# A hybrid encoder block: the order of its stages turned round, input projections first

## The chip, the cores and the metric

The kernel runs on one core of a Trainium2 chip. The metric is the device time in microseconds of one execution. TensorE (PE) multiplies, VectorE (DVE), ScalarE (ACT) and GpSimd (POOL) do the elementwise work, SyncE (SP) issues the weight loads. Each engine works through its own instruction stream; semaphores join them.

## The reference, cut to what matters

One residual block on x of 512 tokens by 2048 features, in float32:

```
h    = rms_norm(x, norm_g)
proj = h @ w_in          # split into c, b, u, conv_z (1024 each), c_q 512, c_kv 512, k_rope 64,
                         # mla_z 2048, mem_q 1024, mem_z 1024, g_conv, g_mla, g_mem (2048 each)
o_conv = (b * conv3(c * u) * silu(conv_z)) @ w_conv_out
q  = rms_norm(c_q) @ w_uq;  k, v = rms_norm(c_kv) @ w_ukv      # 16 heads, 128 + 64 rotary
mla_y = attention(q, k, v, chunk mask)
o_mla = (mla_y * silu(mla_z)) @ w_mla_out
mk, mv = rms_norm(mem, mem_norm_g) @ w_mem_kv                  # mem: 256 tokens, 4 heads of 256
mem_y = attention(rms_norm(mem_q), rms_norm(mk), mv)
o_mem = (mem_y * silu(mem_z)) @ w_mem_out
merged = sigmoid(g_conv)*o_conv + sigmoid(g_mla)*o_mla + sigmoid(g_mem)*o_mem
out = x + merged @ w_o
```

## The kernel before

**How a product is made.** Every float32 operand is cut into a high part (`hi`, an ACT copy to the type fp32r, L121) and a low part (`lo`, a DVE subtraction, L123, or with a gain L125). `mm3` (L152 to L154) makes one product of three matmuls: hi by hi, hi by lo, lo by hi. A weight chunk is 256 rows by 512 columns (512 KB, tile `raw`); its cut takes one ACT and one DVE instruction of 128x1024. All sums of a product collect in PSUM banks; there are four under the tag `acc` and four under `aux`.

**Dense products** (`dense_steps`, later `d_group`) take one chunk at a time for four token blocks: 24 matmuls with 512 columns for a chunk, 192 for 512 output columns of a 2048-row weight. The latents c_kv use chunks of 288 columns.

**Block products** (`f_group`, `t_group`) are a two-by-two block scheme with seven products in place of eight (P1 to P7). DVE forms sums and differences of the weight blocks before they are cut, and of the result blocks afterwards. `f_group` gives 512 features by all tokens in 14 steps of 24 matmuls with 256 columns; `t_group` gives 1024 columns by all tokens in 28 steps of 12 matmuls with 512 columns. Both read `BX`, the blocks of the normalised x: their parts `b0` and `b1` and the sums `f`, cut like everything else.

**The stages, in order.**
1. Memory keys and values: `w_mem_kv`, 4 groups of 8 chunks, two token blocks each, so 12 matmuls of 512 columns a chunk. `memory_chunk` loads and cuts mem, `add_squares` on POOL (L241, L245) sums the squares. Meanwhile x is loaded, and `make_hT` scales it on POOL (L303), cuts it (`hT`) and stores it to `hdram`.
2. The latents: `w_ckv0`, `w_ckv1` (288 columns each), `w_cq`, from `hT`.
3. Latent attention: `project` makes keys, values and queries of two heads, `attend` is a generator for one head. The strings `ORDER_FIRST`, `ORDER` and `ORDER_LAST` say in which order a step of `project` (p), of a head (0, 1) or of the previous head (L) is written. The result is copied (L675) to `ydram`.
4. The memory query `w_memq`, a dense product; h comes back from `hdram`. Then memory attention, two heads after each half of the query product (`mem_queries`, `mem_attend`, L742 to L800).
5. `w_memz`, a dense product; `build_x` makes BX between its steps.
6. Block products: 8 conv groups and 4 `w_mlaz` groups (`f_group`; `mlaz_group` multiplies with the attention result from `ydram`, L1176), then 6 gate groups (`t_group`).
7. The output side: `w_mem_out` (dense), `w_mla_out` (block), `w_conv_out` (dense), `w_o` (block).

**What sets the order.** From stage 5 on, `steps` is a list: each step cuts its weights (`forms`), then multiplies, then runs what hangs on it (`after`); the cut of the next step is written ahead of the `after` of this one. On PE, ACT, DVE and POOL a planner orders the instructions at compile time by costs that it simulates, with the written order as priority; SP keeps the written order (`manual_schedule`):

```
ctx.enter_context(tc.manual_schedule(engines={mybir.EngineType.SP}))
...
with tile.TileContext(nc, schedule_with_timeline_sim=True) as tc, ExitStack() as ctx:
```

Tiles of one tag share a few buffers; a write waits until the old content is used.

## Time and profile before

| | us |
|---|---|
| median of 3 runs | 2172.26 (2170.84 to 2175.69) |
| the profiled execution, time | 2173.34 |
| its span, first to last instruction | 2171.5 |
| PE busy | 2120.9 |
| weight loads of PE busy | 1857.2 |
| DVE busy | 1586.1 |
| ACT busy | 1024.2 |
| POOL busy | 213.1 |

The span is what the engines took from the first instruction to the last; the time holds 1.8 us more around it. A busy time is the time in which at least one instruction of the engine ran, so span less busy is idle time. A row of stretches gives the length, then for each engine the busy time and the count of instructions, then the granted clock of PE as a share of full speed, the busy share of the DMA engines, and what they moved.

### The profile page before, as it was taken

What the parts mean: (1) busy time and instruction counts of PE and PEld (TensorE: products, weight loads), DVE (VectorE), ACT (ScalarE), POOL (GpSimd) and SP (SyncE); (2) the same over time, 40 slices, a digit from 0 to 9 for tenths busy, and PEclk for the clock granted to TensorE, in tenths of its full rate; (3) what the DMA queues carried; (4) which work ended last, traced back from release to release, by engine and by line L of the source; (5) the groups of instructions that cost most, each with busy time, mean ns of one, the idle gap of its engine ahead of it and who ended that gap; (6) DMA issues with size and microseconds to landing.
All of it is one profiled execution on the core that took longest, in us unless ns stands there. A gap on an engine that the chain in (4) does not pass through costs nothing.

```text
span 2171.5 us, 30437 instructions
## 1 busy us (share of the span) xinstructions
PE 2120.9 (98%) x11832; PEld 1857.2 (86%) x11832; DVE 1586.1 (73%) x2101; ACT 1024.2 (47%) x1509; POOL 213.1 (10%) x211
## 2 busy tenths in 40 slices
PE   6999999999989999999999999999999999999999
PEld 5788888888868899999999988888888888888887
DVE  7863767774457578778777877777787678777986
ACT  5533667675344344444444444444455434443443
POOL 7510311210000000000000000000001100021000
PEclk9999999999999999999999999999999999999999
DMA  7583212234225332332454454544456666585662
GB/s 264 156 258 111 88 49 64 69 127 166 76 70 202 127 116 90 127 122 84 145 165 157 146 181 128 195 164 166 154 204 212 237 240 190 188 243 163 208 230 78
DMA packets 103679, 334.29 MB, mean 154 GB/s; under 512 B 11120, under 2 KB 11376, under 8 KB 103536
## 3 DMA queue, kind: packets, MB, share of 16 engines
q1 hardware_dynamic: 73008, 256.51, 36.0%
q0 software_dynamic: 12864, 43.00, 6.3%
q10 hardware_dynamic: 17664, 32.86, 4.0%
q8 instruction: 92, 1.51, 0.3%
q14 instruction: 51, 0.42, 0.1%
HBM read 284.09 MB, written 48.23 MB: 153 GB/s over the span
## 4 chain that ended last, share of the span: by engine, by line
PE 68%; DVE 1%; issue 1%; DMA 1%; ACT 1%; POOL 0%; ACTq 0%; DVEq 0%; POOLq 0%
PE aux L152 12%; PE aux L154 12%; PE aux L153 12%; PE acc L153 10%; PE acc L154 10%; PE acc L152 10%; DMA araw<-adram 1%; DVE wlo L123 0%; PE aux L203 0%; ACT p L777 0%; PE acc L203 0%; ACT whi L121 0%; DVE qrow L746 0%; POOL mdram L1338 0%; DVE r L1232 0%
## 5 line engine op out<-in xcount | busy, mean ns | idle before, releaser
L121 ACT ACTIVATE whi<-raw 128x1024 fp32r<-128x1024 f32 x472 | 499.8, 1060 | 700.7 <-PE aux L153 310.2
L123 DVE TENSOR_TENSOR wlo<-raw,whi 128x1024 fp32r<-128x1024 f32 x472 | 575.4, 1223 | 277.8 <-ACT whi L121 277.1
L146 DVE TENSOR_TENSOR wlo<-raw,whi 128x1024 fp32r<-128x1024 f32 (+3 forms) x105 | 128.9, 1228 | 112.6 <-ACT whi L145 112.2
L962 DVE TENSOR_TENSOR raw<-raw 128x1024 f32<-128x1024 f32 x160 | 195.6, 1223 | 8.6 <-DMA raw<-in_w_mla_out 2.7
L145 ACT ACTIVATE whi<-raw 128x1024 fp32r<-128x1024 f32 (+3 forms) x105 | 101.2, 964 | 141.0 <-PE acc L154 71.8
L154 PE MATMUL acc<-whi,blk 128*128 128x512 f32 (+1 forms) x384 | 144.4, 377 | 0.0
L153 PE MATMUL acc<-wlo,blk 128*128 128x512 f32 (+1 forms) x384 | 144.2, 376 | 0.0
L152 PE MATMUL acc<-whi,blk 128*128 128x512 f32 (+1 forms) x384 | 142.1, 384 | 2.1 <-DVE qt L584 1.4
L153 PE MATMUL aux<-wlo,f 128*128 128x512 f32 x320 | 124.5, 389 | 0.0
L154 PE MATMUL aux<-whi,f 128*128 128x512 f32 x320 | 124.5, 389 | 0.0
L152 PE MATMUL aux<-whi,f 128*128 128x512 f32 x320 | 113.2, 389 | 0.5 <-ACT E L1366 0.5
L196 POOL TENSOR_TENSOR rs_r<-rs_t,mhalf 128x2 f32<-128x2 f32 (+1 forms) x77 | 69.5, 907 | 287.7 <-DVE rs_t L195 202.2
L908 DVE TENSOR_TENSOR raw<-raw 128x1024 f32<-128x1024 f32 x72 | 87.1, 1222 | 1.4
L152 PEld LDWEIGHTS acc<-whi,blk 128*128 128x128 f32 x384 | 72.4, 189 | 14.2 <-ACT kn L562 2.2
L154 PE MATMUL acc<-f,wlo 128*128 128x256 f32 x288 | 81.6, 283 | 1.6 <-DVE wlo L123 1.6
L153 PE MATMUL acc<-f,whi 128*128 128x256 f32 x288 | 81.5, 283 | 0.0
L152 PE MATMUL aux<-f,whi 128*128 128x256 f32 x288 | 81.5, 283 | 0.0
L153 PE MATMUL aux<-f,whi 128*128 128x256 f32 x288 | 81.5, 283 | 0.0
L154 PE MATMUL aux<-f,wlo 128*128 128x256 f32 x288 | 81.5, 283 | 0.0
L152 PE MATMUL acc<-f,whi 128*128 128x256 f32 x288 | 81.5, 283 | 0.0
L154 PEld LDWEIGHTS acc<-whi,blk 128*128 128x128 f32 x384 | 72.5, 189 | 10.2
L153 PEld LDWEIGHTS acc<-wlo,blk 128*128 128x128 f32 x384 | 72.7, 189 | 9.4
(405 smaller groups left out, 5937.9 us busy)
## 6 DMA issues: line engine op xcount, KB each, us to landing
raw<-in_w_conv SPq DMA_DIRECT2D x64, 512.0 KB, 3.8
raw<-in_w_mla_out SPq DMA_DIRECT2D x44, 512.0 KB, 4.7
raw<-in_w_o SPq DMA_DIRECT2D x44, 512.0 KB, 4.3
raw<-in_w_gmem SPq DMA_DIRECT2D x40, 512.0 KB, 3.6
raw<-in_w_gconv SPq DMA_DIRECT2D x40, 512.0 KB, 3.8
raw<-in_w_gmla SPq DMA_DIRECT2D x40, 512.0 KB, 4.3
raw<-in_w_mlaz SPq DMA_DIRECT2D x32, 512.0 KB, 3.9
raw<-in_w_mem_kv SPq DMA_DIRECT2D x31, 512.0 KB, 3.7
```

Source lines behind the costliest of these rows:

```text
L121: act.activation(hi, src, AF.Copy, scale=1.0 if g is None else g)
L123: vec.tensor_tensor(out=lo, in0=src, in1=r32(hi), op=ALU.subtract)
L145: act.activation(hi[:, cols], raw[:, cols], AF.Copy)
L146: vec.tensor_tensor(out=lo[:, cols], in0=raw[:, cols], in1=r32(hi[:, cols]), op=ALU.subtract)
L152: nc.tensor.matmul(o, lhsT=s[0], rhs=m[0], start=start, stop=False, skip_group_check=shared)
L153: nc.tensor.matmul(o, lhsT=s[0], rhs=m[1], start=False, stop=False, skip_group_check=shared)
L154: nc.tensor.matmul(o, lhsT=s[1], rhs=m[0], start=False, stop=stop, skip_group_check=shared)
L196: pool.tensor_tensor(out=r, in0=t, in1=mhalf[:, :n], op=ALU.pow)
L908: vec.tensor_tensor(out=src_, in0=fetch(i0), in1=fetch(i1), op=op)
L962: vec.tensor_tensor(out=src_, in0=src_, in1=fetch((gid, other, c)), op=op)
```

## The change

The stages stand in a new order, and two products change their kind.

- x is loaded first. Its unscaled chunks, times the gain, are cut (`x_chunk`) and go straight into both c_kv products, interleaved by chunk (`kv_forms`, `kv_products`), and into c_q. The scale of a token is a factor of a whole row of these latents, so it is left out there, and the norms of the latents take a corrected epsilon (`xe`). The latents are stored to `ckvdram`, `krdram`, `cqdram`.
- The sum of squares of x is made by ACT and DVE (`x_squares`), `make_scale` turns it into the scale, and `build_x` makes BX between the steps of c_q, on DVE.
- All block products follow: gate group 0 first (with the `lead` order, in which the fourth chunk comes last; it loads four chunks twice), conv, the other gates, `w_mlaz`, and now also `w_memz` (`f_group`) and `w_memq` (`t_group`), which were dense. Their results go to DRAM (`zdram`, `mzdram`, `mqdram`).
- Memory keys and values come next; the memory tokens are loaded and cut during the last gate group (`mem_load`, `mem_cut`, `mem_sum`). The four memory heads are generators now, and their parts hang between the 32 steps (`go`), as do the rotary tables, the loads of the latents and their scales.
- Then latent attention. `attend` loads its gate z (POOL queue) and multiplies the result with it on DVE in place of the ACT copy; `mlaz_group`'s multiplication is gone.
- The last heads are interleaved with the first steps of `w_mem_out` instead of with the memory query.
- `hdram`, `ydram`, `mydram` and their transfers are gone. Weights of all stages share one ring (`w`, ten buffers; before, four in the first stages).

The diff, cut to its core:

```diff
-    making = make_hT()
-    for grp in range(4):
-        banks = [bank("acc") for _ in range(2)]
-        for c, _ in enumerate(dense_steps(banks, a["w_mem_kv"][grp], 512, mT, "T", nk=KB, cut=grp == 0,
-                                          before=memory_chunk if grp == 0 else None)):
...
+    def x_chunk(c):
+        t = xraw[c] = q("xraw")
+        hi, lo = (blk("xhi"), blk("xlo")) if c < 4 else (b1("xhi"), b1("xlo"))
...
+        for k in range(KC):
+            split(t[:, k], hi[:, k], lo[:, k], g(G_NORM + KC * c + k))
+            hx[KC * c + k] = (hi[:, k], lo[:, k])
+    def x_squares(c):
+        sq = q("sq")
+        act.activation(flat(sq), flat(xraw[c]), AF.Square)
+        if c:
+            vec.tensor_tensor(out=flat(xacc[0]), in0=flat(xacc[0]), in1=flat(sq), op=ALU.add)
...
+    for c in range(8):
+        for n in range(2):
+            steps.append(Step(lambda n=n, c=c: kv_forms(n, c), [lambda ws, n=n, c=c: kv_products(ws, n, c)],
+                              [lambda n=n: kv_results(n)] if c == 7 else []))
...
+    def build_x(c):
+        for j in (c, c + 4):
+            for k in range(KC):
+                t = xraw[j][:, k]
+                vec.scalar_tensor_tensor(out=t, in0=t, scalar=g(G_NORM + KC * j + k), in1=scale[0],
+                                         op0=ALU.mult, op1=ALU.mult)
+        build(BX, c, xraw[c], xraw[c + 4], blk)
+    first = len(steps)
+    after(first - 1, make_scale)
+    d_group(a["w_cq"], hx, "aux", q_results, "F", order=(0, 4, 1, 5, 2, 6, 3, 7))
+    for c in range(4):
+        after(first + 2 * c + 1, lambda c=c: build_x(c), True)
...
+    gate_group(0, 0, True)
+    for cb in range(8):
+        f_group(a["w_conv"][cb], BX, conv_group(cb), "aux" if cb % 2 else "acc")
+    gate_group(0, 1)
+    for grp in range(4):
+        f_group(a["w_mlaz"][grp], BX, z_group(zdram, 4 * grp), "aux" if grp % 2 else "acc")
+    gate_group(1, 0)
+    gate_group(1, 1)
+    for grp in range(2):
+        f_group(a["w_memz"][grp], BX, z_group(mzdram, 4 * grp), "aux" if grp % 2 else "acc")
+    t_group(a["w_memq"][0], BX, rows_group(mqdram, 0, AF.Copy))
+    gate_group(2, 0)
+    last_s = len(steps)
+    gate_group(2, 1)
...
+    for grp in (0, 2, 1, 3):
+        d_group(a["w_mem_kv"][grp], mT, "acc", mem_results(grp), "T", nb=2)
+    after(first_m - 1, mem_sum)
...
+    def mem_attend(head):
+        rows = pq.tile([P, NTB, M], F32, tag="rows", name="rows", bufs=2)
+        nc.gpsimd.dma_start(rows, mqdram[:, :, head * M:(head + 1) * M].rearrange("t p f -> p t f"))
+        yield
...
+    for s, h in ((0, 0), (1, 0), (2, 1), (8, 0), (9, 1), (11, 0), (12, 1), (14, 1), (16, 0), (17, 1), (17, 2), (18, 3),
+                 (19, 2), (24, 2), (25, 3), (27, 2), (28, 3), (30, 3)):
+        after(first_m + s, go(h))
+    for s, f in ((3, rotary_tables), (20, latent_loads), (22, key_scales), (23, key_rotary), (26, query_scale)):
+        after(first_m + s, f)
...
+    query_blocks()
+    for h in range(2, 4):
+        for _ in heads_m[h]:
+            pass
+    key_blocks()
...
+    run_all(queries(0, res0))
+    run_all(keys_values(0, res0, "aux"))
...
     def attend(head, h, qrb, res):
+        z = pa.tile([P, S], F32, tag="z", name="z", bufs=3)
+        nc.gpsimd.dma_start(z, zdram[head])
...
-        y = pa.tile([P, S], F32, tag="y", name="y", bufs=2)
-        act.activation(y, yb, AF.Copy)
-        (nc.gpsimd if head >= HEADS - 4 else nc.scalar).dma_start(ydram[head], y)
+        vec.tensor_tensor(out=z, in0=yb, in1=z, op=ALU.mult)
+        (nc.gpsimd if head >= HEADS - 4 else nc.scalar).dma_start(adram[16 + head], z)
...
+    late_steps = run_range(first_o, len(steps))
+    a0, a1 = prev
+    run(*[{"p": late_steps, "L": late, "0": a0, "1": a1}[c] for c in ORDER_LAST])
...
-    a["w_memq"] = groups(w_in, 7232, 1024)
-    a["w_memz"] = groups(w_in, 8256, 1024)
+    a["w_memq"] = two_by_two_t(w_in[:, 7232:8256])[None]
+    a["w_memz"] = np.stack([two_by_two(w_in, [(8256 + i * 512, 512)]) for i in range(2)])
```

## The prediction

> **What bounds the kernel now.** I read the page first: busy times, then the chain that ended last.

> ```profile
> span 2171.5 us, 30437 instructions
> PE 2120.9 (98%) x11832; PEld 1857.2 (86%) x11832; DVE 1586.1 (73%) x2101; ACT 1024.2 (47%) x1509; POOL 213.1 (10%) x211
> PE 68%; DVE 1%; issue 1%; DMA 1%; ACT 1%; POOL 0%; ACTq 0%; DVEq 0%; POOLq 0%
> ```

> PE is the bound. It is idle for 2171.5 - 2120.9 = 50.6 us, so a reordering can win at most that plus whatever PE work it removes. The view of stretches, cut at the stages, shows where the idle time lies:

> ```profile
> core 0: us, PE busy (x) PEld busy (x) DVE busy (x) ACT busy (x) POOL busy (x), PEclk, DMA share, GB/s
> 0.00:36.00 36.00, 21.83 (x82) 16.33 (x82) 28.15 (x29) 18.64 (x29) 23.37 (x20) 0.95 0.72 258
> 36.00:117.00 81.00, 72.89 (x324) 56.17 (x324) 66.76 (x63) 46.97 (x71) 49.98 (x28) 1.00 0.58 185
> 117.00:160.00 43.00, 41.53 (x291) 39.60 (x290) 24.95 (x54) 15.47 (x28) 3.19 (x2) 1.00 0.85 274
> 208.00:470.00 262.00, 256.39 (x1416) 226.43 (x1415) 189.31 (x556) 177.26 (x430) 56.88 (x62) 0.99 0.21 68
> 470.00:565.00 95.00, 91.78 (x484) 78.66 (x483) 49.53 (x131) 50.26 (x123) 11.28 (x14) 1.00 0.48 169
> 613.00:648.00 35.00, 25.22 (x117) 19.32 (x116) 19.45 (x46) 14.41 (x43) 4.27 (x6) 0.85 0.21 70
> 648.00:736.00 88.00, 87.27 (x385) 72.27 (x386) 51.29 (x68) 32.32 (x45) 3.37 (x5) 1.00 0.50 179
> 736.00:1059.00 323.00, 321.44 (x2679) 321.24 (x2678) 259.30 (x256) 141.18 (x153) 0.99 (x2) 1.00 0.36 114
> ...
> 1378.00:1531.00 153.00, 153.00 (x677) 126.69 (x676) 118.13 (x107) 72.71 (x75) 0.00 (x0) 1.00 0.50 167
> 1922.00:2012.00 90.00, 89.16 (x418) 74.20 (x417) 62.12 (x71) 35.13 (x45) 9.95 (x13) 1.00 0.63 209
> 2012.00:2171.50 159.50, 154.34 (x688) 127.16 (x686) 129.34 (x124) 66.30 (x71) 5.78 (x8) 1.00 0.51 172
> ```

> Length less PE busy, from the top: 14.2, 8.1, 1.5 (memory keys, then latents), 5.6 (latent attention), 3.2 (its end), 9.8 (the last two memory heads), 0.7, 1.6, 0, 0.8, 5.2 (output side and tail). Together 50.7: all of it. The clock column adds a loss that busy time hides: 25.22 x 0.15 + 21.83 x 0.05 = 4.9 us at a lower clock. Who PE waited for:

> ```profile
> PE acc L153 <- DVE wlo L146: 17.0, 16, 4.2
> PE acc L152 <- ACT whi L145: 6.8, 4, 5.8
> PE aux L203 <- DVE p L782: 4.2, 4, 1.9
> PE aux L203 <- DVE qrow L746: 2.4, 3, 1.3
> ```

> The largest is the weight cut at the start, the others are memory heads that stand alone. Why DVE is late there, its timeline and POOL's say:

> ```profile
> 17.95 2.06 DVE L146 TENSOR_TENSOR wlo<-raw,whi 128x1024 fp32r<-128x1024 f32 x1
> 30.36 1.21 DVE L146 TENSOR_TENSOR wlo<-raw,whi 128x1024 fp32r<-128x1024 f32 x1
> 18.89 3.67 POOL L245 TENSOR_TENSOR macc<-macc,sq 128x512 f32<-128x512 f32 x2
> ```

> The same cut takes 2.06 us while POOL sums squares and 1.21 us after it has stopped.

> **PE work.** Matmuls of 512 columns follow each other every 87.27/385 = 0.2267 us (the memory gate's stretch; 153/677 = 0.226 in the gates'), those of 256 columns every 321.44/2679 = 0.120. The memory gate `w_memz` goes from 2 x 192 x 0.2267 = 87.0 to 2 x 336 x 0.120 = 80.6: **-6.4**. The memory query goes from 87.0 to 336 x 0.2267 = 76.2: **-10.9**. An eighth less work gives the gate only a fourteenth, because in the conv stretch the weight loads (PEld) are busy for 321.24 of 323 us: with 256 columns a matmul is paced by its weights. [...] The scales of memory and of the latent queries take eight one-column matmuls more:

> ```profile
> 35.30 0.95 PE L264 MATMUL aux<-one,macc 128*128 128x1 f32 x8
> ```

> That is +0.9. All other products keep count and shape. Work: **-16.4**.

> **The start.** One 256 KB transfer, one cut, one matmul, as before: 5.8 us idle (the 5.8 of L145) stays. Then per chunk PE has 48 matmuls of 288 columns, started here nine matmuls apart:

> ```profile
> 129.87 0.30 PE L154 MATMUL acc<-whi,hT 128*128 128x288 f32 x1
> ...
> 131.05 0.29 PE L153 MATMUL acc<-wlo,hT 128*128 128x288 f32 x1
> ```

> That is 0.131 each, 6.3 us a chunk. It loads 1.1 MB, 174 GB/s, where 117 to 160 us moved 274 at 1.5 us of PE idle. DVE prices:

> ```profile
> L123 DVE TENSOR_TENSOR wlo<-raw,whi 128x1024 fp32r<-128x1024 f32 x472 | 575.4, 1223 | 277.8 <-ACT whi L121 277.1
> L123 DVE TENSOR_TENSOR f<-t,f 128x512 fp32r<-128x512 f32 x36 | 23.9, 686 | 0.1
> L146 DVE TENSOR_TENSOR wlo<-raw,whi 128x576 fp32r<-128x576 f32 x16 | 12.1, 757 | 24.2 <-ACT whi L145 24.1
> L1160 DVE SCALAR_TENSOR_TENSOR r<-cu,gains,r 128x512 f32<-128x512 f32 x8 | 6.0, 746 | 0.0
> ```

> DVE needs 2 x 0.746 + 2 x 0.757 + 1.22 = 4.2 us a chunk, without POOL beside it: hidden. I take 0.5 idle (0 to 4).

> **c_q and BX.** PE has 192 x 0.2267 = 43.5 us. DVE has four builds, each 4 x 0.746 (scale) + 4 x 0.69 (sums) + 2 x 1.22 + 3 x 0.686 (cuts) = 10.2, and eight weight cuts: 50.6. It starts some 5 us late, behind the chain sum, power, transposes, copy; three cuts are made ahead (six buffers). DVE then runs about 50.6 + 5 - 3.7 - 43.5 = 8 us past PE, and steps queued behind a build (the third, fifth, seventh cut) hold PE. The lead order, which wants the fourth chunk last, gives some back. Lower end 0 if the planner puts cuts ahead of builds, upper end 12; I take **5**. Before, the builds lay in the memory gate's 87 us with 51.29 of DVE: free.

> **Block groups.** Gate groups (DVE 118.13 of 153) and conv (259.30 of 323) ran with 0 and 1.6 idle and keep their form; `w_mlaz` loses its multiplications. 1.6 stays.

> **Memory stage.** 32 steps are 384 x 0.2267 = 87.1 of PE. A head is 24 x 0.120 + 12 x 0.2267 + 16 transposes. Rows that price heads:

> ```profile
> 579.32 1.04 PE L203 MATMUL aux<-ident,p 128*128 128x128 f32 x8
> L195 DVE TENSOR_SCALAR rs_t<-ss,ke 128x2 f32<-128x2 f32 x32 | 7.3, 242 | 0.3
> L771 DVE TENSOR_REDUCE mx<-aux 128x2 f32<-128x512 f32 x8 | 5.5, 690 | 4.4 <-PE aux L154 4.3
> 565.00:613.00 48.00, 48.00 (x248) 40.85 (x248) 18.99 (x34) 17.81 (x37) 0.00 (x0) 1.00 0.12 39
> ```

> So 7.7 us a head, 118 for the stage. DVE: cuts 39; a head 1.22 + 2 x (0.75 + 0.69 + 0.69 + 0.34 + 0.69 + 0.69) = 8.9, so 36; keys and values 12; tables and scales some 70 small ones at about 0.24 = 17: 104, or 88%. From 565 to 613 two heads lay between dense steps with no PE idle, but steps there last twice as long. Lower end 0, upper end 12 (1.22 x 10 late cuts); I take **4**, for 9.8 before.

> **Into latent attention.** All eight `blk` tiles hold memory features until the last memory step, so the latents' cuts wait for it; and the keys of groups 0 and 1 share the four `aux` banks, so the second waits for an eviction through ACT, DVE and POOL. Cover is the last heads' 24 matmuls (5.4 us) and 16 transposes (2.1). 0 to 10, taken: **5**. Before, this seam was free.

> **Latent attention and its end.** The gate's multiplication adds 16 x 0.69 = 11 to DVE: 200 of 262, still covered. Sixteen z loads join POOL's queue; the powers queue behind each, and DVE's normalisation waits for those:

> ```profile
> L1093 POOL DMA_DIRECT2D adram<-y x4 | 2.9, 728 | 75.0 <-DVE y L1092 75.0
> L196 POOL TENSOR_TENSOR rs_r<-rs_t,mhalf 128x2 f32<-128x2 f32 x44 | 35.4, 811 | 151.4 <-DVE rs_t L195 149.8 <-ACT sq L243 1.3
> ```

> 16 x 0.73 = 12 us on an engine busy for 57 of 262: PE idle stays 5.6. The end, now against `w_mem_out`: 2.5 for 3.2 (0 to 7). Output side and tail: 0.8 + 5.2. SP is moved past nothing it waits for: its loads have ten buffers in place of four, and 16.8 MB to and from `hdram` are gone.

> **The sum.** Idle after: 5.8 + 0.5 + 5 + 1.6 + 4 + 5 + 5.6 + 2.5 + 0.8 + 5.2 = 36.0, for 50.6: -14.6. Lower clock: 4.9 before, an estimate of 1.5 after (one start): -3.4. Work -16.4. Together -34.4: span 2137.1, and 1.8 around it (2173.34 - 2171.5) 2138.9. The profiled run lies 1.1 above the median of the runs, so **2138**.

> **Rivals.** *The seams close*: the planner fills all five new seams (0.5, 5, 4, 5, 2.5): 2138 - 17 - 1.5 of clock = 2119. For it: 565 to 613. Against it: DVE at 50.6 for 43.5 in c_q is no matter of order. *The seams gape*: c_q 10, memory 12, the two ends 10 and 5, so 20 more: 2158; or 34 more, no change, 2172. For it: 9.8 idle in 35 us at memory heads. *Slower*: POOL and DVE disturb each other in the memory stage, as from 17.95 to 22 us. DVE is at 104 for PE's 118, so a slowdown beyond 1.13 decides; at 2.06/1.21 = 1.7 it takes 177, 59 more: 2197. [...] Against it: only about 20 us of POOL (powers and DMA issues at 0.73 to 0.81) lie in those 118 us, and conv's cuts kept 1.22 beside loads. The break-even with 2172 is a slowdown of 1.46. That the products stay dense is ruled out by the diff.

> **How the numbers follow.** Forecast 0.50, seams close 0.15, seams gape but less than the gain 0.20, gain eaten 0.06, slower 0.09. The range 2117 to 2164 leaves out the last two and a little of each edge. A measurement here tells 0.2% (4.3 us) from no change; so faster 0.85, same 0.06, slower 0.09.

> **What would show it.** Right: conv-like pitch (0.120) in `w_memz`; first cuts at 1.22; PE idle under 10 us up to the end of c_q beyond the start; a memory stage near 118 us. Wrong: cuts of 2 us in the memory stage, a PE wait over 5 us on the first gate group, or a clock under 0.9 at the seam into latent attention.

## The result, and the profile after

The changed kernel takes 2153.68 us (median of 4 runs, 2153.02 to 2155.12) where the kernel before took 2171.99 beside it (4 runs, 2170.84 to 2175.69): a ratio of 0.9914, 95% interval 0.9897 to 0.9931. It is faster by 18.3 us. The forecast was 34.4 us faster, at 2138; the time lies inside the range of 2117 to 2164. The profiled execution took 2154.08 us, with a span of 2152.3.

The head of the page after, busy times and chain:

```profile
span 2152.3 us, 31076 instructions
PE 2104.1 (98%) x12088; PEld 1863.5 (87%) x12088; DVE 1639.6 (76%) x2169; ACT 1058.5 (49%) x1529; POOL 148.0 (7%) x183
PE 90%; DVE 3%; issue 3%; ACT 2%; DMA 1%; POOL 0%; DVEq 0%; POOLq 0%; ACTq 0%
```

PE busy fell from 2120.9 to 2104.1, by 16.8. Its idle time hardly fell: 2152.3 - 2104.1 = 48.2 us, for 50.6. The view of stretches after, cut at the new stages (length, busy time and count for PE, weight loads, DVE, ACT, POOL, then the granted clock, DMA share and GB/s):

```profile
0.00:36.00 36.00, 29.16 (x200) 29.16 (x201) 26.27 (x41) 26.22 (x39) 1.44 (x6) 1.00 0.83 299
36.00:102.00 66.00, 66.00 (x380) 59.13 (x379) 41.30 (x57) 24.45 (x35) 1.03 (x1) 1.00 0.40 136
102.00:165.00 63.00, 54.03 (x228) 43.90 (x227) 51.33 (x53) 30.39 (x37) 0.00 (x0) 0.95 0.41 134
165.00:1190.00 1025.00, 1020.80 (x6714) 941.45 (x6713) 790.49 (x750) 476.62 (x510) 2.19 (x4) 1.00 0.43 143
1190.00:1310.00 120.00, 120.00 (x585) 100.86 (x584) 92.29 (x162) 74.22 (x143) 24.00 (x27) 1.00 0.62 214
1345.00:1440.00 95.00, 82.44 (x411) 70.23 (x410) 60.82 (x171) 51.55 (x128) 22.38 (x26) 0.93 0.26 89
1440.00:1480.00 40.00, 39.77 (x229) 35.22 (x228) 30.67 (x90) 28.09 (x68) 8.33 (x11) 1.00 0.21 73
1480.00:1575.00 95.00, 91.34 (x510) 79.27 (x509) 75.21 (x223) 64.13 (x157) 22.05 (x27) 1.00 0.23 74
1575.00:1640.00 65.00, 62.30 (x350) 55.91 (x349) 52.50 (x153) 44.91 (x110) 15.15 (x16) 0.97 0.29 98
1640.00:1710.00 70.00, 66.88 (x341) 56.31 (x341) 38.64 (x77) 32.32 (x62) 10.58 (x16) 1.00 0.48 173
1710.00:1995.00 285.00, 283.53 (x1272) 234.11 (x1271) 223.35 (x233) 118.93 (x133) 33.34 (x41) 1.00 0.65 212
2135.00:2152.30 17.30, 12.83 (x57) 10.30 (x55) 9.08 (x10) 2.29 (x3) 0.00 (x0) 1.00 0.23 91
```

Length less PE busy: 6.8 up to 36 us, then nothing up to 102; 9.0 where the first gate group begins; 4.2 in the block groups after that; 0 from 1190 to 1310, at the end of the block groups and in the memory stage; 12.6 where latent attention begins, 0.2 and 3.7 later in it; 2.7 and 3.1 at its end; 1.5 and 4.5 on the output side and in the tail. The old start with its memory keys and latents, 23.8 us of idle time before, became 6.8; the last two memory heads, 9.8 when they stood alone, became none. Most of it came back at two seams that the new order made: 9.0 between c_q and the gate groups, and 12.6 on the way into latent attention. There the clock is lower as well, 0.95 and 0.93. Whom PE waited for after (us in total, times, longest):

```profile
PE aux L143 <- DVE ptl L119: 7.0, 4, 2.7
PE aux L127 <- ACT whi L117: 6.8, 1, 6.8
PE aux L127 <- ACT cq L558: 6.6, 1, 6.6
PE acc L127 <- ACT whi L117: 5.5, 2, 4.4
```

The second is the first cut of the kernel. The others are new: a copy of c_q (third), a weight cut at the seam into latent attention (fourth), and the cuts of transposed weights in attention (first). The 4.2 us in the block groups are three waits of 1.4 for a weight cut, one each time that 256-column products follow a gate group. The first of them:

```profile
199.28 0.39 PE L129 MATMUL acc<-f,wlo 128*128 128x256 f32 x1 [1.40 <-DVE wlo L119]
```

**The first seam.** The timeline after, where the first gate group needs the `aux` banks (start, length, instruction, idle time before it and its releaser):

```profile
106.28 0.39 PE L129 MATMUL aux<-xhi,wlo 128*128 128x512 f32 x1
...
115.35 0.50 PE L129 MATMUL acc<-whi,b 128*128 128x512 f32 x1 [2.33 <-DVE b L119]
118.69 1.22 DVE L358 TENSOR_TENSOR raw<-raw 128x1024 f32<-128x1024 f32 x1
120.00 1.06 ACT L117 ACTIVATE whi<-raw 128x1024 fp32r<-128x1024 f32 x1 [7.02 <-DVE raw L358]
123.47 1.55 ACT L558 ACTIVATE cq<-aux 128x512 f32<-128x512 f32 x3
124.10 0.80 PE L127 MATMUL aux<-whi,f 128*128 128x512 f32 x1 [6.64 <-ACT cq L558]
```

The products of c_q end at 106.7 us, and in them PE had no idle time. PE goes on with the gate group in the `acc` banks, waits there 2.33 us for a cut of x by DVE (`b`), and stands still for 6.64 us when it needs the `aux` banks. The copy of c_q out of these (L558) starts at 123.47. ACT was idle for 7.02 us ahead of that, held by a weight cut that needs a sum of DVE's (L358); the copy, which needed nothing any more, stood behind it in ACT's stream.

**The second seam.** The same view where latent attention begins:

```profile
1361.74 0.17 DVE L1045 MEMSET zero<- 128x128 f32 x1 [5.28 <-DMA adram<-z]
1361.94 0.31 ACT L1131 ACTIVATE pt30h<-zero 128x128 fp32r<-128x128 f32 x1 [5.74 <-DVE zero L1045]
1370.11 0.96 PE L127 MATMUL acc<-whi,cqT 128*128 128x384 f32 x4 [4.42 <-ACT whi L117]
```

The fill of a constant tile of zeros (L1045) waits until the result `z` of a memory head has been stored; so the tile seems to lie in memory that the head used, though the trace shows no addresses. DVE stands for 5.28 us and ACT, which copies from it, for 5.74, while the first queries and keys lie in their banks; PE then waits 4.42 us for a cut that is late by that. It is the longest of the waits that make up the 12.6 us; those for the cuts of transposed weights (3.8) and of queries (2.3) are most of the rest.

### The profile page after: what moved, and what is told of

The parts are those of the page before. It is cut to its first block, busy times and chain, and to the rows that moved or that the text cites. A ratio compares the mean times of both kernels' runs of the same rounds, so it can differ in the third digit from the quotient of the medians.

```text
span 2152.3 us, 31076 instructions
## 1 busy us (share of the span) xinstructions
PE 2104.1 (98%) x12088; PEld 1863.5 (87%) x12088; DVE 1639.6 (76%) x2169; ACT 1058.5 (49%) x1529; POOL 148.0 (7%) x183
## 4 chain that ended last, share of the span: by engine, by line
PE 90%; DVE 3%; issue 3%; ACT 2%; DMA 1%; POOL 0%; DVEq 0%; POOLq 0%; ACTq 0%
PE aux L127 15%; PE aux L128 14%; PE aux L129 14%; PE acc L127 14%; PE acc L128 14%; PE acc L129 14%; PE aux L143 1%; DVE wlo L119 1%; DMA araw<-adram 1%; PE aux L1184 1%; PE aux L1167 0%; PE aux L1164 0%; PE aux L1168 0%; PE aux L1166 0%; DMA adram<-z 0%
## 5 line engine op out<-in xcount | busy, mean ns | idle before, releaser
L117 ACT ACTIVATE whi<-raw 128x1024 fp32r<-128x1024 f32 (+3 forms) x598 | 621.3, 1041 | 822.3 <-PE aux L128 357.0
L119 DVE TENSOR_TENSOR wlo<-raw,whi 128x1024 fp32r<-128x1024 f32 (+3 forms) x598 | 714.8, 1200 | 342.3 <-ACT whi L117 337.2
L358 DVE TENSOR_TENSOR raw<-raw 128x1024 f32<-128x1024 f32 x176 | 215.0, 1223 | 9.8 <-DMA raw<-in_w_gmla 2.6
L129 PE MATMUL acc<-whi,b 128*128 128x512 f32 x352 | 136.9, 389 | 2.3 <-DVE b L119 2.3
L128 PE MATMUL aux<-wlo,b 128*128 128x512 f32 x352 | 137.1, 389 | 0.0
L129 PE MATMUL aux<-whi,b 128*128 128x512 f32 x352 | 136.9, 389 | 0.0
L128 PE MATMUL acc<-wlo,b 128*128 128x512 f32 x352 | 136.9, 389 | 0.0
L127 PE MATMUL acc<-b,whi 128*128 128x256 f32 x448 | 126.9, 283 | 0.0
L129 PE MATMUL acc<-b,wlo 128*128 128x256 f32 x448 | 126.8, 283 | 0.0
L127 PE MATMUL aux<-b,whi 128*128 128x256 f32 x448 | 126.8, 283 | 0.0
L128 PE MATMUL aux<-b,whi 128*128 128x256 f32 x448 | 126.8, 283 | 0.0
L129 PE MATMUL aux<-b,wlo 128*128 128x256 f32 x448 | 126.8, 283 | 0.0
L128 PE MATMUL acc<-b,whi 128*128 128x256 f32 x448 | 126.8, 283 | 0.0
L127 PE MATMUL acc<-whi,b 128*128 128x512 f32 x352 | 124.2, 390 | 0.0
L127 PE MATMUL aux<-whi,b 128*128 128x512 f32 x352 | 122.8, 389 | 0.0
L304 DVE TENSOR_TENSOR raw<-raw 128x1024 f32<-128x1024 f32 x84 | 101.8, 1223 | 1.7
```

What stands on the lines that cost most here:

```text
L117: act.activation(hi, src, AF.Copy, scale=1.0 if g is None else g)
L119: vec.tensor_tensor(out=lo, in0=src, in1=r32(hi), op=ALU.subtract)
L127: nc.tensor.matmul(o, lhsT=s[0], rhs=m[0], start=start, stop=False, skip_group_check=shared)
L128: nc.tensor.matmul(o, lhsT=s[0], rhs=m[1], start=False, stop=False, skip_group_check=shared)
L129: nc.tensor.matmul(o, lhsT=s[1], rhs=m[0], start=False, stop=stop, skip_group_check=shared)
L304: vec.tensor_tensor(out=src_, in0=fetch(i0), in1=fetch(i1), op=op)
```

## The experiments

The kernel before ran beside each group of them, at 2174.07 (13 runs), 2173.74 and 2173.97 us (9 runs each).

**1. The copies of c_q earlier.** `build_x` hangs on steps of c_q with a flag that writes it ahead of what else hangs there. For the fourth build the flag is taken away, so the copies of c_q are written ahead of it. Nothing else changes.

```diff
-        after(first + 2 * c + 1, lambda c=c: build_x(c), True)
+        after(first + 2 * c + 1, lambda c=c: build_x(c), c < 3)
```

> The c_q results are written ahead of the fourth build of BX instead of behind it. In the changed kernel PE stands still for 6.6 us on the first gate group until ACT has copied c_q out of the aux banks, and runs at a lower clock after it. Theory 'late copy' (the copy is queued behind the build and a weight cut that waits for DVE): the copy runs within 5 us of the last c_q product, PE idle from 102 to 165 us falls from 9.0 to under 3 us, the span by 6 to 10 us. Rival 'DVE backlog' (the forecast's step: builds and cuts together are more than PE's work there): PE waits for DVE's cuts instead, and the span falls by less than 3 us.

Measured: 2141.68 us (4 runs), ratio 0.9849 (0.9831 to 0.9867), 12.0 us below the changed kernel, 11.1 by the spans. Stretch and copy with this edit:

```profile
102.00:165.00 63.00, 61.20 (x266) 49.09 (x265) 57.32 (x60) 34.37 (x40) 0.00 (x0) 1.00 0.49 168
111.34 1.54 ACT L558 ACTIVATE cq<-aux 128x512 f32<-128x512 f32 x3
```

The copy starts 12 us sooner, PE's idle time in the stretch is 1.8 us for 9.0, and the clock is 1.00 for 0.95. DVE has the same builds to make. So 7.2 of the 9.0 us were a matter of order, as the theory 'late copy' had it; 1.4 of what is left is a wait for DVE's cut of `b`.

**2. The constants at the start.** The tiles of zeros and of reciprocals (`zero`, `invd`) are made among the constants at the beginning and keep memory of their own.

```diff
+    invd, zero = const.tile([P, 4], F32, name="invd"), const.tile([P, P], F32, name="zero")
+    vec.memset(invd[:, 0:2], 1.0 / 128); vec.memset(invd[:, 2:4], 1.0 / 64); vec.memset(zero, 0.0)
...
-    invd = pp.tile([P, 4], F32, name="invd")
...
-    zero = pp.tile([P, P], F32, name="zero")
-    vec.memset(zero, 0.0)
```

> The two constant tiles zero and invd of latent attention are made at the kernel's start, so that their memory is no longer that of the memory heads. In the changed kernel DVE stands for 5.3 us behind the clearing of zero, which waits for the last memory head's store. Theory 'reused memory': without that wait the evictions of the first queries and keys start 5 us earlier, PE idle from 1345 to 1440 us falls from 12.6 to about 7, the span by 4 to 8 us with the clock. Rival 'shared banks' (the forecast's step: keys of groups 0 and 1 share the aux banks, eviction through ACT, DVE and POOL sets the pace): the wait goes elsewhere, the span falls by less than 2 us.

Measured: 2149.72 us (4 runs), ratio 0.9887 (0.9867 to 0.9906). That is 4.0 below the changed kernel, but the interval overlaps with its own (0.9897 to 0.9931), so the time alone doesn't settle it. In the trace, DVE's wait for the store is gone, PE's idle time from 1345 to 1440 us goes from 12.6 to 9.5 (the theory had about 7), and the wait for the weight cut there from 4.4 to 2.2.

**3. Memory gate and memory query dense again.** In the new order, `w_memz` and `w_memq` are dense products as before. They read the tiles that the block scheme holds, so the numbers of memory gate and query, and of what depends on them, are not the reference's; count and shape of the products are those of before.

```diff
-        f_group(a["w_memz"][grp], BX, z_group(mzdram, 4 * grp), "aux" if grp % 2 else "acc")
-    t_group(a["w_memq"][0], BX, rows_group(mqdram, 0, AF.Copy))
+        d_group(a["w_memz"][grp], dense_x, "aux" if grp % 2 else "acc", dz(grp), "F")
+    for grp in range(2):
+        d_group(a["w_memq"][grp], dense_x, "aux" if grp % 2 else "acc", dq(grp))
```

> The changed kernel with memory gate and memory query as dense products again, 192 matmuls of 512 columns for 512 outputs. They read the whole cut tiles that hold the blocks of x; half of the even tiles holds a sum of blocks instead of x by then, so the kernel's memory branch computes other numbers, with the same work. Theory 'by the rows' (0.2267 us for 512 columns, 0.120 for 256): 17.3 us slower than the changed kernel, 6.4 from the gate and 10.9 from the query. Rival 'an eighth each' (a 256-column matmul costs half of a 512-column one once the weight loads are hidden): 21.8 slower. Rival 'nothing' (DVE or transfers set the pace there): under 5 slower.

Measured: 2168.63 us (10 runs), ratio 0.9977 (0.9968 to 0.9987): 15.0 us above the changed kernel by the medians, 16.9 by the spans (the execution that was profiled is the slowest of the ten). PE busy with this edit:

```profile
PE 2121.0 (98%) x11848; PEld 1862.9 (86%) x11848; DVE 1560.9 (72%) x2094; ACT 1031.7 (48%) x1505; POOL 147.1 (7%) x183
```

2121.0 - 2104.1 = 16.9: the two products in blocks save what the rows gave (6.4 + 10.9 = 17.3). This is most of what the whole change gained: the new order with dense products is only 5.4 us faster than the kernel before (2168.63 for 2174.07).

**4. Latent attention without its gate.** The loads of z and the multiplication with it are left out, and ACT copies the result as before; so the output lacks the gate of latent attention.

```diff
-        nc.gpsimd.dma_start(z, zdram[head])
...
-        vec.tensor_tensor(out=z, in0=yb, in1=z, op=ALU.mult)
+        act.activation(z, yb, AF.Copy)
```

> Latent attention without its gate: no load of z on POOL's queue and an ACT copy in place of the DVE multiplication, as in the kernel before; the multiplication with the gate is left out of the computation. PE idle from 1362 to 1710 us is 22 us in the changed kernel, for 8.8 in the same stages before. Theory 'the gate costs' (DVE 11 us busier, 16 loads ahead of the powers on POOL): idle in the stage falls by 8 to 12 us, the span by 8 to 14. Rival 'order' (the planner's order of the stage's first and last group, and the wait at its start): idle and span fall by less than 4 us.

Measured: 2147.32 us (4 runs), ratio 0.9874 (0.9853 to 0.9895), 6.4 us below the changed kernel, between what the two theories gave. The seam is as it was (12.5 us of idle time from 1345 to 1440); from 1480 to 1640 it falls from 6.4 to 3.0, and the waits for the cuts of transposed weights from 7.0 to 3.6. The next two kernels split it.

**5. The loads of z through ACT's queue.** The multiplication stays.

```diff
-        nc.gpsimd.dma_start(z, zdram[head])
+        nc.scalar.dma_start(z, zdram[head])
```

> The gates of the latent heads are loaded through ScalarE's queue instead of GpSimd's; the multiplication stays. It splits what leaving both out gained (6.4 us). Theory A (VectorE's multiplication is the cost): nothing changes, 2152 to 2155, the waits for the cuts of the transposed weights stay at 7.0 us. Theory B (the loads hold GpSimd, which makes the scales that the keys wait for): 2147 to 2149.

Measured: 2153.07 us (4 runs), ratio 0.9901 (0.9887 to 0.9915): nothing that can be told from the changed kernel, and the waits for the cuts stay at 6.9 us. POOL's queue, which the prediction charged with 12 us off the path, is off it.

**6. The multiplication on POOL.** ACT copies the result out of its bank (a tile `y` more), and POOL multiplies.

```diff
-        vec.tensor_tensor(out=z, in0=yb, in1=z, op=ALU.mult)
+        y = pa.tile([P, S], F32, tag="y", name="y")
+        act.activation(y, yb, AF.Copy)
+        pool.tensor_tensor(out=z, in0=y, in1=z, op=ALU.mult)
```

> The multiplication of each latent head's output by its gate goes from VectorE to GpSimd (after a copy out of the bank by ScalarE); all else as in the changed kernel. Theory A (VectorE's queue is what TensorE waits for in the last head groups, through the cuts of the transposed weights): as with the multiplication left out, 4 to 6 us off the 2153.7, some 2148 to 2150, with the waits for those cuts near 3.6 instead of 7.0 us. Theory B (the slower rival of the prediction: GpSimd's two-input operations slow VectorE's beside them, as the cuts of 2.06 against 1.21 us at the start of the kernel before): 16 multiplications that each cover one or two cuts give back 16 times 0.85 us of VectorE's time or more, so no gain, 2153 to 2160, and VectorE's cuts of 0.48 us beside them show 0.8.

Measured: 2144.21 us (4 runs), ratio 0.9863 (0.9849 to 0.9877): 9.5 us below the changed kernel, more than with the multiplication left out. It is below what either theory gave, so the multiplication on DVE isn't the whole cause, and the trace names another. Timeline of this kernel:

```profile
1312.71 0.17 DVE L1045 MEMSET zero<- 128x128 f32 x1
```

The tile of zeros is filled 49 us sooner and waits for no store. Nothing in the edit touches it; that the tile `y` has shifted others in memory, so that it lies elsewhere, is the likely reason, but not shown. From 1345 to 1440 us PE is idle for 8.1 us instead of 12.6, as the constants at the start had it (9.5); from 1480 to 1640 it is 5.4, not the 3.0 of experiment 4. So 4.5 us of idle time, where the spans differ by 7.2, are the second seam's, come by without being sought.

**7. Both orders mended.** Experiments 1 and 2 together.

> Both edits together: the latents' results ahead of the fourth build of x, and the constants made at the start. Theory A (the two losses lie in different places and add): 12.0 and 4.0 us off the 2153.7 of the changed kernel, 2137.7; the wait of 4.0 us for the weight cut at the seam into latent attention falls below 2.5 and VectorE's idle time of 4.83 us for the store of a memory head is gone. Theory B (the 4.0 of the constants was the planner's order falling differently, not the wait): no better than 2141, with the idle time of TensorE between 1340 and 1440 us as it was with the first edit alone. Theory C (the work comes earlier than its data, and a new wait opens in the block groups): above 2143.

Measured: 2137.02 us (5 runs), ratio 0.9833 (0.9819 to 0.9846), 16.7 us below the changed kernel: the two add, as theory A had it. The page:

```profile
span 2135.1 us, 31076 instructions
PE 2099.4 (98%) x12088; PEld 1860.3 (87%) x12088; DVE 1639.1 (77%) x2169; ACT 1058.0 (50%) x1529; POOL 147.8 (7%) x183
```

Idle time is 2135.1 - 2099.4 = 35.7 us, and PE is busy for 4.7 us less than in the changed kernel with the same matmuls, 2.7 of it because the clock no longer falls at the first seam (1.00 for 0.95 over 54.03 us).

**8. All three.** Experiments 1, 2 and 6 together.

> The three edits together: the latents' results ahead of the fourth build of x, the constants made at the start, the multiplication by the latent gates on GpSimd. Theory A (three losses in three places, each with its own price: 16.7 us for the first two together, 9.5 for the third, against the changed kernel): 2153.7 - 16.7 - 9.5 = 2127.5. Theory B (the gain of the third edit is in part the same idle time of the seam into latent attention, where the waits for the cuts of weights fell with it from 5.5 to 1.9 us): 2130 to 2134. Theory C (with the others in place GpSimd's multiplications are late for the scales of the keys): 2136 or more.

Measured: 2137.76 us (5 runs), ratio 0.9831 (0.9818 to 0.9844): the same as experiment 7. The sum of the parts (2127.5) fails, and the time is that of theory C. Its cause isn't, as far as the trace tells: PE waits for no scale of POOL's, only 2.1 us for ACT's copy into `y`. The wait that the third edit took away at the second seam is one that the second edit takes away as well; where the rest of its 9.5 us went, the runs don't show. From 1480 to 1640 us 5.8 us stay idle here, for 5.2 in experiment 7; freeing DVE of 16 multiplications gained nothing there.

**9. The kernel before without POOL's sums.** Squares on ACT and sums on DVE (L241, L245). It asks what the old order lost at the start.

```diff
-        if eng is pool:
-            pool.tensor_tensor(out=sq, in0=t, in1=t, op=ALU.mult)
-        else:
-            act.activation(sq, t, AF.Square)
+        act.activation(sq, t, AF.Square)
         if c:
-            pool.tensor_tensor(out=acc, in0=acc, in1=sq, op=ALU.add)
+            vec.tensor_tensor(out=acc, in0=acc, in1=sq, op=ALU.add)
```

> The kernel before, with the squares of memory and x made by ScalarE and summed by VectorE instead of GpSimd. Theory A (VectorE's cuts take 2.06 to 2.29 instead of 1.21 us at the start of the kernel before because GpSimd's squares and sums run beside them): cuts near 1.21 us in the first 30 us although VectorE now has more to do; TensorE's idle time of 11.9 us in the first 20 us falls by 2 to 5 us, and the time is 2168 to 2175 (the sums on VectorE cost back some of it). Theory B (the cuts are slow for another reason, the loads that arrive at 255 to 281 GB/s): cuts stay above 1.9 us, and the time is 2174 to 2182.

Measured: 2162.55 us (4 runs), ratio 0.9946 (0.9932 to 0.996), 11.2 us below the kernel before and below what either theory gave. First the kernel before, then this one, over the first 100 us, with a weight cut of this one:

```profile
0.00:100.00 100.00, 80.85 (x346) 62.12 (x346) 78.39 (x80) 56.50 (x88) 61.67 (x40) 0.98 0.64 217
```

```profile
0.00:100.00 100.00, 88.68 (x389) 70.07 (x390) 79.73 (x102) 65.62 (x103) 28.59 (x22) 1.00 0.66 233
17.03 1.22 DVE L146 TENSOR_TENSOR wlo<-raw,whi 128x1024 fp32r<-128x1024 f32 x1
```

The cuts take 1.22 us for 2.06 although DMA brings more (233 GB/s for 217), so the loads don't slow them and POOL's sums do. PE is idle for 7.8 us less in 100. A part of what the old order lost at its start was thus not the order's: it could have been had by moving the sums alone. Measured against this kernel, the new order without the block products (experiment 3, 2168.63) is 6 us slower.

## Why the prediction was right in sign and missed half of the size

Sign and range came out right by the two terms that make most of the gain, the block products and the start; the seams failed.

| term, idle time in us | forecast | after |
|---|---|---|
| start and c_kv | 5.8 + 0.5 | 6.8 |
| c_q and BX, up to 165 us (the first gate group runs on to 194) | 5 | 9.0 |
| block groups after that | 1.6 | 4.2 |
| memory stage | 4 | 0 |
| into latent attention, and in it | 5 + 5.6 | 12.6 + 0.2 + 3.7 |
| its end | 2.5 | 2.7 + 3.1 |
| output side and tail | 0.8 + 5.2 | 1.5 + 4.5 |
| sum | 36.0 | 48.2 |

*Work, -16.4: right.* Experiment 3 gives 16.9 for the two products; with the 0.9 for small matmuls, that is -16.0.

*The start: right.* 23.8 us of idle time became 6.8 for a forecast of 6.3, and cuts at the start no longer share their time with POOL, which is busy for 1.44 us there. Experiment 9 shows POOL's sums as the cause of some 10 of the 23.8: without them the old order has 14.2 us of idle time up to 160 us. Part of the rest may be POOL's scaling of x, which stays in that kernel and beside which cuts of `hT` take 1.77 us for 0.74; that wasn't tried.

*c_q and BX, 5: wrong in place and in most of the cause.* The prediction wrote that DVE's 50.6 us for PE's 43.5 is "no matter of order" and looked for the idle time within c_q. Within c_q there was none. Only the 2.3 us that PE waited for DVE's cut of `b`, in the gate group, are of the kind that it had in mind. The other 6.6 came because, when c_q was done, its copies stood behind the last build and a weight cut in ACT's stream, on banks that the gate group needs. Experiment 1 moves one call and takes 7.2 of the 9.0 us away, with DVE's load as it was. So it was a matter of order, and the step that failed is the comparison of two engines' totals where the question was who holds the banks. The sign named for it, a PE wait over 5 us on the first gate group, did appear, at 6.6.

*Block groups, 1.6: too low.* The 1.6 of before was one wait for a weight cut, where the dense memory gate passes into the 256-column groups. The prediction kept it, but the new order has three such passages, and PE waits 1.4 us at each. In experiment 3, with two, it waits 2.8.

*Memory stage, 4: too high.* From its first step on PE was never idle:

```profile
1222.60:1340.00 117.40, 117.40 (x613) 100.43 (x612) 91.97 (x176) 76.45 (x162) 21.61 (x23) 1.00 0.61 204
```

DVE was busy for 92 us there (104 forecast). The slower rival asked for cuts stretched 1.46-fold by POOL, and the weight cuts of this stage took 1.23 us at most; POOL was busy for 22 us.

*Into latent attention, 5: too low, and the longest wait not foreseen.* The prediction named held `blk` tiles and shared `aux` banks. PE's longest wait, 4.4 of the 12.6 us, was for a cut behind DVE's wait for a DMA, over a tile of constants that reuses memory; the diff shows that tile unmoved, and only the stage ahead of it is new. Without that wait PE's idle time from 1345 to 1440 us is lower by 3.0 us in experiment 2, by 4.5 in 6, and by 2.7 in 7 (8.8, for 11.5 in 1). Whether the tiles and banks that the prediction named make up what is left wasn't tried. Its other sign, a clock under 0.9 at this seam, came too (0.81 from 1362 to 1380 us).

*Latent attention, 5.6 unchanged: too low.* With both seams mended, 8.8 us remain from 1345 to 1440 and 4.5 up to 1575: 13.3 in all, for 10.6 forecast for the seam and the stage together. The waits for the cuts of transposed weights are part of it, as this timeline of experiment 7 shows:

```profile
1396.52 0.96 DVE L119 TENSOR_TENSOR wlo<-raw,whi 128x768 fp32r<-128x768 f32 x1 [1.59 <-ACT whi L117]
1398.12 1.22 DVE L119 TENSOR_TENSOR wlo<-raw,whi 128x1024 fp32r<-128x1024 f32 x1 [0.64 <-ACT whi L117]
1399.59 1.47 DVE L119 TENSOR_TENSOR ptl<-aux,pth 128x512 fp32r<-128x512 f32 x3
1400.32 0.66 PE L143 MATMUL aux<-ident,kn 128*128 128x128 f32 x4 [2.67 <-DVE ptl L119]
```

Two weight cuts for the next products stand ahead of the cuts that would free the banks. Before, PE's longest wait for these cuts was 0.9 us. Whether the larger ring of weights (ten buffers for four) lets such cuts go ahead wasn't tried. Experiment 4 leaves the share of the gate open, at most 6.4 us; moving it off DVE gained nothing in the end (8).

*Its end, 2.5: too low,* with 2.7 + 3.1. No run was aimed at it; in experiments 1 and 7, which edit nothing there, the 2.7 are 0.9.

*Lower clock, -3.4: wrong.* One stretch at a lower clock was forecast and three came: 54.03 x 0.05 + 82.44 x 0.07 + 62.30 x 0.03 = 10.3 us. The 4.9 counted before left out latent attention (256.39 x 0.01, 2.6 us more), so the loss grew by some 2.8 where it was to fall by 3.4. Work and clock together then give a fall of PE busy by 16.0 - 2.8 = 13.2. It fell by 16.8, and no run explains the 3.6 between them (the clock column is rounded to 0.01, so they are rough); that the 19.8 forecast was missed by only 3.0 is partly luck.

Idle time 12.2 and busy time 3.0 above the forecast make the 15.2 us by which the span missed (2152.3 for 2137.1). Experiment 7 lies at 2135.1 with 35.7 us idle; that it meets the forecast's 36.0 is partly chance, since latent attention has more idle time than forecast and the memory stage less.

## What to carry to other kernels

When stages change places, list for each new seam which banks and which memory the next stage takes over, and which instruction, in which engine's stream, gives them back; totals of busy time per engine don't see this. An engine that works through its stream in order can stand idle with ready work behind one late instruction, as ACT did here for 7.02 us ahead of the copy of c_q, so look at what stands ahead of the copy that frees a bank, and keep small constants out of memory that is used in turn. An edit can take away a wait that it has nothing to do with, as one more tile did here: look for the wait in the trace before crediting the edit.

## What the runs showed of the hardware beyond that

```profile
124.69 0.63 PE L128 MATMUL aux<-wlo,f 128*128 128x512 f32 x1
125.12 0.63 PE L129 MATMUL aux<-whi,f 128*128 128x512 f32 x1
...
129.03 0.40 PE L127 MATMUL aux<-whi,f 128*128 128x512 f32 x1
129.26 0.39 PE L128 MATMUL aux<-wlo,f 128*128 128x512 f32 x1
```

Matmuls of 512 columns start 0.43 us apart up to 128.5 and 0.23 apart from then on, so 4.4 us run at half speed; the granted clock is 0.97 from 118 to 122 us, 0.50 from 122 to 128 and 0.85 from 128 to 130. An estimate from these three puts the fall 4.3 us after the stand began (117.5) and the rise 4.5 us after it ended (124.1). In experiment 7 a stand of only 2.67 us (the last row of its timeline above) is followed by 256-column matmuls 0.215 us apart instead of 0.120:

```profile
1404.00:1405.00 1.00, 1.00 (x6) 1.00 (x6) 0.13 (x1) 0.00 (x0) 0.00 (x0) 0.50 0.00 0
1404.21 0.42 PE L1167 MATMUL aux<-krh,qr 128*128 128x256 f32 x1
1404.42 0.41 PE L1168 MATMUL aux<-krl,qr 128*128 128x256 f32 x1
```

PE was not quite still after that stand: of the 4 us from 1398 to 1402 it was busy for 1.12, with transposes. Ahead of the stand matmuls of 512 columns started 0.23 us apart (at 1395.68 and 1395.91 us); from 1404 to 1405 the clock is 0.50. So here the clock was lost after a stand of 2.67 us, with little work after it.

**Where POOL slowed DVE, and where it didn't.** Two of the 16 multiplications on POOL in experiment 6 and the DVE instructions that run beside them; the cuts `ptl` have one input in a bank, `qb` has both in SBUF:

```profile
1422.15 1.27 POOL L1201 TENSOR_TENSOR z<-y,z 128x512 f32<-128x512 f32 x1 [9.53 <-ACT y L1200]
1422.64 1.49 DVE L119 TENSOR_TENSOR ptl<-aux,pth 128x512 fp32r<-128x512 f32 x3 [1.97 <-ACT pth L117]
...
1449.19 0.42 DVE L951 TENSOR_TENSOR qb<-qt,sinq 128x256 f32<-128x256 f32 x1
1449.35 1.41 POOL L1201 TENSOR_TENSOR z<-y,z 128x512 f32<-128x512 f32 x1 [1.48 <-ACT y L1200]
1449.53 1.52 DVE L952 TENSOR_TENSOR qb<-qt,sinq 128x256 f32<-128x256 f32 x1
```

The three cuts take 1.49 us together, 0.78 of it beside POOL, as without POOL (1.47 in the timeline of experiment 7). The second `qb` takes 1.52 us where the one before it, of the same shape, took 0.42, and it ends 0.3 us after POOL's multiplication; in the changed kernel all eight of this line take 0.42. The first `qb` was there before POOL and keeps its time, the second began beside it. These two are the only DVE instructions with two SBUF inputs, columns of scalars not counted, that run beside any of the 16 multiplications for more than 0.1 us. So if such instructions are the ones that POOL slows, as these rows suggest and no run tested, the slowdown that theory B of experiment 6 had in mind found little to act on. The slow weight cuts at the start of the kernel before read two tiles in SBUF too: 2.06 us beside POOL's sums, 1.21 after them.
